# Convolution taps of a gated MLP: from an SBUF copy of the up-projection to the PSUM accumulator itself

## The chip, the cores and the metric

The kernel runs on one core of a Trainium2 chip. The core has five engines that run side by side and wait for each other on semaphores: TensorE (matrix products, into PSUM), VectorE, ScalarE and GpSimd (elementwise work) and SyncE (here: the queue that issues the DMA transfers). The profile calls them PE, DVE, ACT, POOL and SP; PEld is the loading of TensorE's weights. PSUM is TensorE's output memory; it has eight banks, and one bank holds a 128 x 512 float32 tile. GpSimd has no path to PSUM in this kernel: all that it reads lies in SBUF.

The metric is the device time of one execution in microseconds. Three runs of the kernel before gave 3285.91, 3288.57 and 3295.32 us; the median is 3288.57 us.

## The reference, cut to what matters

One layer: a mixer sub-layer (Fourier transform and gated linear recurrence, not touched here) and a gated MLP with a depthwise 3 x 3 convolution. The change lies in the MLP, which in the reference is

```python
def conv_ffn(h, w_up, conv_w, conv_b, w_down, rows, cols):
    b, l, _ = h.shape                                        # 2048 tokens = 32 rows x 64 columns
    z = (h @ w_up).reshape(b, rows, cols, 2 * D_FF)          # 1024 -> 5632 channels
    z = lax.conv_general_dilated(z, conv_w[:, :, None, :], window_strides=(1, 1), padding='SAME',
                                 dimension_numbers=('NHWC', 'HWIO', 'NHWC'),
                                 feature_group_count=2 * D_FF)   # each channel by itself
    z = z.reshape(b, l, 2 * D_FF) + conv_b
    return (jax.nn.silu(z[..., :D_FF]) * z[..., D_FF:]) @ w_down   # 2816 -> 1024
```

Its output is scaled, added to the stream and normed. All is float32.

## The kernel before

Every large product is taken in three matmuls: both operands are split into a rounded high part (a ScalarE cast, L102) and a remainder (a subtraction, L103, on GpSimd or VectorE), and hi*hi, hi*lo and lo*hi are summed in PSUM (`mm3`, L140 to L147). `load_w` (L130) brings a 1024 x 128 column tile of a weight matrix in two halves: for each half a DMA into a staging tile `rw` (two buffers), a cast and a GpSimd subtraction. The split weights have two buffers (`w`), so a weight tile can be prepared while TensorE uses the one before.

Phase 3 (`phase3`, L933) is the up-projection with the convolution. Its input, `h2`, lies in SBUF, channels on the partitions, in four blocks of 512 tokens. The 5632 channels are worked off in 44 tiles of 128: for each j from 0 to 21 first channel tile j (half 0, the part that goes through Silu) and then channel tile j + 22 (half 1, the factor). One channel tile is

- 96 matmuls (4 token blocks x 8 slices of the 1024 inputs x 3) into `z`, 128 channels x 2048 tokens, four banks of PSUM. Half 0 uses the pool `za`, half 1 `zb`, one tile each, so that TensorE can write one while the other is read.
- on ScalarE the copy `zs` of all four banks to SBUF (L952, two buffers) and from `zs` the centre tap with the bias, into `ac` (L953, three buffers).
- on VectorE the other eight taps (`conv`, L967): eight multiply-add instructions (L979), each reading a shifted view of `zs` and adding to `ac` in place.

After both halves `gate` (L961) applies Silu to `ac` of half 0 on ScalarE (L963), multiplies both halves on GpSimd (L964) and stores the product to DRAM (`dZ[j]`). For the last j, Silu, product and store are written later, in the loop of `down`, and the product is on VectorE.

`down` (L982) is the down-projection: two halves of 512 output channels times four blocks of 512 tokens, eight groups of 22 x 12 matmuls. A group sums into four tiles `dn` of one bank each, from a pool of its own that is opened when the two pools of `z` have closed. In the first group, each of its 22 steps loads and splits both a weight tile (`wd`, into the SBUF slots H0 to H5 that held `h2`) and a tile of `dZ` (`gh`, `gl`, three buffers); the weights stay for the next three groups.

Each engine works off its own queue strictly in order. That order isn't the order of the program text: a planner walks through the traced instructions with estimated durations, and puts onto each engine the earliest-traced instruction that is ready in its estimate. An instruction whose input comes later than estimated holds up all that stands behind it on its engine. `tc.issue_after(x)` adds a fixed order behind the instruction x.

Of the kernel before, what the change touches and what calls it, by code (L numbers as in the profile page):

```python
"""FNet / HGRN2 / ConvFFN hybrid layer on one Trainium2 core.

The large matrix products run in float32r: every float32 operand is split exactly into a high
part (12 significant bits) and the remainder, and hi*hi + hi*lo + lo*hi is accumulated in PSUM.
The HGRN2 recurrence runs over windows of 128 tokens; inside a window the decays between two
tokens are products of per-block prefix and suffix products at dyadic block sizes (all factors
are at most one), one product per level, merged by level masks. The FNet position transform is
a 16 x 128 factorization: 16-point transforms on VectorE, twiddled 128-point ones on TensorE.
"""
# [8 lines left out]
F32 = mybir.dt.float32  # L18
# [12 lines left out]
NB = 4            # 512-token blocks  # L31
TB = 512
KD = D // P       # 8
DFF = 2816
NF = DFF // P     # 22
# [10 lines left out]
def constants():  # L46
    """Arrays that depend on the shapes alone."""
    n2 = np.arange(128)
    # level masks: entry (s, t) belongs to the level whose block size first separates s and t
# [5 lines left out]
    cmask = np.stack(lev, 1)                       # [s, 8, t]  # L55
    # twiddled 128-point transforms, one table for each residue k1
# [13 lines left out]
    ch = np.stack([np.cos(ang), np.sin(ang)], 1) / 512.0             # [c, 2, c']  # L70
    eye = np.eye(128)
    rst = np.zeros((128, 640))
    rst[:, 127::128] = 1.0                                           # where the scans restart
# [5 lines left out]
def fap(t, off, dims):  # L79
    """Access pattern over the free elements of a whole tile."""  # L80
    a = t[:]
    return bass.AP(a.tensor, a.offset + off, [list(a.ap[0])] + [list(q) for q in dims])


class Banks:
    """PSUM tiles from the pool that holds their tag."""
# [8 lines left out]
class Layer:  # L95
# [3 lines left out]
    # ------------------------------------------------------------------ helpers  # L99
    def split(self, hi, lo, raw, eng=None):  # L100
        """hi = raw rounded to 12 bits, lo = raw - hi."""
        self.nc.scalar.copy(hi, raw)  # L102
        (eng or self.nc.gpsimd).tensor_tensor(lo, raw, hi, op=SUB)  # L103

    def load_split(self, hi, lo, src, eng=None, pool=None, bufs=2):
        """Load [128, n] or [128, k, c] float32 data of at most 512 columns and split it."""
# [10 lines left out]
    def rsqrt(self, pool, v, n):  # L117
        """v ** -0.5 for positive v of shape [128, n]: bit-level guess and three Newton steps."""
# [11 lines left out]
    def load_w(self, ap, name):  # L130
        """A [1024, 128] column tile of a weight matrix -> hi, lo tiles [128, 8, 128]."""
# [8 lines left out]
    def mm3(self, ps, pairs, start=True, stop=True):  # L140
        """Accumulate the products of the (lhs_hi, lhs_lo, rhs_hi, rhs_lo) in pairs."""
# [7 lines left out]
    # ------------------------------------------------------------------ the layer  # L149
# [44 lines left out]
    # ------------------------------------------------------------------ phase 1  # L194
    def phase1(self):
# [6 lines left out]
        self.mod_A = pc.tile([P, KD], F32, name="mod_A")       # norm1_g * (1 + scale)  # L202
# [17 lines left out]
        # the projections fill TensorE between the small products of the two branches  # L220
# [21 lines left out]
    def drain(self):  # L242
        """Trace the rest of the filler's first part and go on to the next."""
        for _ in self.filler.pop(0):
            pass

    def project_all(self, h):
        """The projections of head h for the state passes; from the second head on, with parts of the
        later modulations."""
# [8 lines left out]
    def vec_rows(self, p0):  # L258
        """Small vectors, loaded as rows of 128 and turned into columns."""
# [17 lines left out]
    def startup(self, p0):  # L277
        nc, a = self.nc, self.a
        ps = self.ps
        # silu(c), silu(c_ctx) as columns  # L280
# [7 lines left out]
        # weights of the FNet channels; one half sits where the context goes later  # L288
# [9 lines left out]

        # shift and scale of the first sub-layer, for latents and context: silu(c)^T @ ada_w; the last
        # 512 columns by VectorE, the others by TensorE  # L300
# [45 lines left out]
        # token tiles -> modulated, transposed, split; the products of a block follow the transposes of  # L346
        # the next one
# [24 lines left out]
        # softmax over the two rows of hg_lb, first row  # L372
# [14 lines left out]
        # conv taps as columns  # L387
# [10 lines left out]
    def load_x(self, p0, blk):  # L398
        """The token tiles of a block, each token scaled to unit mean square."""
# [19 lines left out]
    def modulate_steps(self, pool, xs, A, B, hi, lo, tags, every):  # L419
        """[tok, d] tiles -> transposed h = x * A[d] + B[d], split into hi and lo [d, 8, tok]."""  # L420
# [23 lines left out]
    def fill(self, n):  # L444
        """Trace up to n steps of the projections that wait in self.filler; a context in which
        TensorE's instructions are queued behind them."""
        mm = None
        for _ in range(n):
            mm = next(self.filler[0], None) or mm
        return self.tc.issue_after(mm.ins) if mm else nullcontext()  # L450

    def project_steps(self, kind, h):
        """One 128-channel tile of x @ w_in (channel-major), with its activation, to DRAM, in steps
        of three products."""
# [29 lines left out]
    # ------------------------------------------------------------------ FNet branch  # L484
# [9 lines left out]
    def fnet(self, p1, g):  # L494
        nc, a, ps = self.nc, self.a, self.ps
        X = p1.tile([P, 2, TB], F32, name="fX", tag="fX")           # blocks 0, 1 (later G0, G2)
        EF = p1.tile([P, 4, TB], F32, name="fE", tag="fE")          # e, f, g, h
        H = p1.tile([P, 16, P], F32, name="fH", tag="fH")

        U = p1.tile([P, 2, TB], F32, name="fU", tag="fU")           # blocks 2, 3  # L500
# [5 lines left out]
        # 4-point transforms over a (n1 = 4a + b); index b inside the 512 columns  # L506
        v.tensor_tensor(X[:, 0, :], EF[:, 0, :], EF[:, 1, :], op=ADD)      # G_b[0]
        v.tensor_tensor(X[:, 1, :], EF[:, 0, :], EF[:, 1, :], op=SUB)      # G_b[2]
        G0 = X[:, 0, :].rearrange("p (b c) -> p b c", b=4)
        G2 = X[:, 1, :].rearrange("p (b c) -> p b c", b=4)  # L510
        gg = EF[:, 2, :].rearrange("p (b c) -> p b c", b=4)                # Re G_b[1]
        hh = EF[:, 3, :].rearrange("p (b c) -> p b c", b=4)                # -Im G_b[1]
        S = EF[:, 0:2, :].rearrange("p x (b c) -> p (x b) c", b=4)         # scratch, 8 slots
        # H slots: 0,1: k=0,8;  2,3: k=4 (re, -im); 4,5: k=2; 6,7: k=6; 8,9: 1; 10,11: 5; 12,13: 9; 14,15: 13
        # residue 0
# [4 lines left out]
        # residue 2: X2 = G0 + r(G1-G3) - i(G2 + r(G1+G3)), X6 = G0 - r(G1-G3) - i(r(G1+G3) - G2)  # L520
# [7 lines left out]
        # residue 1: W_b = (g - i h)(cos - i sin), b = 0..3, planes re, im in W  # L528
        W = H[:, 8:16, :].rearrange("p (x b) c -> p x b c", x=2)           # [re|im][b]
# [8 lines left out]
        Sv = S.rearrange("p (q x) c -> p q x c", q=4)                      # q: A, D, C, E ; x: re, im  # L538
# [4 lines left out]
        Hk = H[:, 8:16, :].rearrange("p (k x) c -> p k x c", x=2)          # k: 1, 5, 9, 13  # L543
# [7 lines left out]
        Y = EF                                                             # e .. h are no longer needed  # L551
# [526 lines left out]
```

## Time and profile before

| what | value |
|---|---|
| median of three runs | 3288.57 us (3285.91 to 3295.32) |
| the profiled execution: span from its first to its last instruction | 3293.7 us (its own device time isn't listed beside it; the span stands within the three runs' times) |
| busy TensorE / VectorE / ScalarE / GpSimd | 3128.3 / 2007.5 / 933.0 / 957.0 us |
| mean granted TensorE clock | 0.979 of full speed |
| phase 3: first matmul of `z` to start of its last | 1699.6 to 2760.2 us |
| down-projection: start of its first and of its last L1020 matmul | 2781.5 to 3280.4 us |

How to read the lines shown below: a group row gives line, engine, operation, output <- inputs, shapes and count, then busy time and the mean duration in ns, then the idle time just before these instructions and who ended it. A row of one source line gives count, least/median/largest duration in ns, and the first and last start. A timeline row gives start and duration in us, engine, line, operation, count, and in brackets the idle time before it and who ended it. A row of stretches gives from:to, the length, then busy us and instruction counts (x) of PE, PEld, DVE, ACT and POOL, the granted clock, the DMA share and GB/s; an instruction that crosses an edge is counted in both stretches. A matmul row of 0.39 us overlaps its neighbours: the distance of two starts is what one costs.

### The profile page before, as it was taken

To read this page: it belongs to the slowest core of one execution; us is meant where nothing else is said; L and a number is where in the kernel's file an instruction comes from. 1 tells how busy PE (TensorE), PEld (TensorE's weight loads), DVE (VectorE), ACT (ScalarE), POOL (GpSimd) and SP (SyncE) were. 2 spreads that over 40 slices of the span, in tenths; PEclk is the share of its full clock that TensorE was granted. 3 is DMA by queue.
4 is the path that set the end of the run, shared out by engine and by line. 5 is a ranking of instruction groups with operands and counts; after the bars stand their busy time and mean duration, and the time that the engine had idled before them with its cause. 6 is when DMAs were issued, how large, how long until landed. Compare 5 with 4: busy or idle time off the path is not lost.

```text
span 3293.7 us, 38879 instructions
## 1 busy us (share of the span) xinstructions
PE 3128.3 (95%) x14955; PEld 2576.7 (78%) x14955; DVE 2007.5 (61%) x2538; ACT 933.0 (28%) x1498; POOL 957.0 (29%) x514
## 2 busy tenths in 40 slices
PE   7999999999999999999999999999999997999998
PEld 4977788888888888777778777777777776788886
DVE  5355543576666611566458988988988999302324
ACT  3322112233333321333232222222122122323322
POOL 2200110000000011345333434334343343544443
PEclk8999999999999999999999999999999998999999
DMA  6255654423323234555531111101111112534643
GB/s 223 85 166 182 196 166 138 134 95 102 106 90 105 86 111 145 187 165 183 178 110 36 58 36 52 48 32 51 45 36 48 45 46 72 192 121 155 220 147 131
DMA packets 278506, 372.59 MB, mean 113 GB/s; under 512 B 20253, under 2 KB 154289, under 8 KB 274993
## 3 DMA queue, kind: packets, MB, share of 16 engines
q1 hardware_dynamic: 278321, 370.11, 34.3%
q8 instruction: 118, 1.93, 0.2%
q14 instruction: 67, 0.55, 0.1%
HBM read 268.58 MB, written 101.45 MB: 112 GB/s over the span
## 4 chain that ended last, share of the span: by engine, by line
PE 49%; DVE 31%; DMA 8%; issue 5%; ACT 3%; POOL 3%; SPq 0%; ACTq 0%; DVEq 0%; POOLq 0%
DVE ac L979 27%; PE pj L145 8%; PE pj L144 8%; PE pj L146 8%; PE dn L1022 4%; PE dn L1020 4%; PE dn L1021 4%; PE pa L773 3%; ACT ac L953 1%; DMA rw<-in_w_out_dram 1%; DMA rw<-in_w_b_dram 1%; POOL wab L103 1%; PE wo L906 1%; PE wo L908 1%; PE wo L907 1%
## 5 line engine op out<-in xcount | busy, mean ns | idle before, releaser
L979 DVE SCALAR_TENSOR_TENSOR ac<-zs,cw,ac 128x1953 f32<-128x1953 f32 (+2 forms) x352 | 970.2, 2761 | 105.9 <-ACT ac L953 95.3
L146 PE MATMUL z<-h,w_up 128*128 128x512 f32 x1408 | 565.3, 402 | 58.4 <-POOL w_up L103 58.4
L144 PE MATMUL z<-h,w_up 128*128 128x512 f32 x1408 | 560.9, 398 | 1.9 <-DVE mt L912 1.9
L145 PE MATMUL z<-h,w_up 128*128 128x512 f32 x1408 | 560.2, 398 | 0.0
L146 PEld LDWEIGHTS z<-h,w_up 128*128 128x128 f32 x1408 | 272.1, 193 | 126.1 <-POOL w_up L103 69.3
L103 POOL TENSOR_TENSOR w_up<-rw,w_up 128x512 fp32r<-128x512 f32 x88 | 267.5, 3058 | 348.6 <-ACT w_up L102 348.5
L103 POOL TENSOR_TENSOR gl<-rw,gh 128x512 fp32r<-128x512 f32 x176 | 244.4, 1391 | 272.3 <-ACT gh L102 266.0
L144 PEld LDWEIGHTS z<-h,w_up 128*128 128x128 f32 x1408 | 272.6, 194 | 59.2 <-issue 2.3
L145 PEld LDWEIGHTS z<-h,w_up 128*128 128x128 f32 x1408 | 272.0, 193 | 58.4
L1020 PE MATMUL dn<-wd,gh 128*128 128x512 f32 x704 | 278.7, 396 | 22.0 <-ACT zs L952 20.9
L1022 PE MATMUL dn<-wd,gl 128*128 128x512 f32 x704 | 278.9, 396 | 4.0 <-POOL gl L103 4.0
L1021 PE MATMUL dn<-wd,gh 128*128 128x512 f32 x704 | 278.1, 395 | 0.0
L964 POOL TENSOR_TENSOR ac<-ac 128x2048 f32<-128x2048 f32 x21 | 138.8, 6609 | 274.8 <-DVE ac L979 274.8
L102 ACT CAST gh<-rw 128x512 fp32r<-128x512 f32 x176 | 109.1, 621 | 350.9 <-PE dn L1021 219.4
L952 ACT COPY zs<-z 128x2048 f32<-128x2048 f32 x44 | 82.3, 1872 | 392.2 <-PE z L146 392.2
L479 ACT ACTIVATE ev<-pj 128x512 f32<-128x512 f32 (+1 forms) x136 | 79.8, 587 | 354.0 <-PE pj L146 326.3
L1020 PEld LDWEIGHTS dn<-wd,gh 128*128 128x128 f32 x704 | 133.1, 189 | 54.0 <-ACT zs L952 21.3
L1038 DVE TENSOR_TENSOR dtmp<-dn,m 128x512 f32<-128x512 f32 x32 | 21.6, 685 | 247.2 <-PE dn L1022 247.1
L1022 PEld LDWEIGHTS dn<-wd,gl 128*128 128x128 f32 x704 | 133.0, 189 | 38.2 <-POOL gl L103 7.7
L1021 PEld LDWEIGHTS dn<-wd,gh 128*128 128x128 f32 x704 | 133.0, 189 | 30.5
L773 PEld LDWEIGHTS pa<-bQ,bkc 128*128 128x128 f32 x896 | 120.7, 191 | 16.8 <-issue 10.4
L773 PE MATMUL pa<-bQ,bkc 128*128 128x128 f32 x896 | 127.5, 286 | 1.2
(303 smaller groups left out, 6105.8 us busy)
## 6 DMA issues: line engine op xcount, KB each, us to landing
rw<-dZ SPq DMA_DIRECT2D x176, 256.0 KB, 3.1
rw<-in_ffn_up_dram SPq DMA_DIRECT2D x88, 256.0 KB, 3.0
dZ<-ac SPq DMA_DIRECT2D x22, 1024.0 KB, 3.9
rw<-in_w_in_dram SPq DMA_DIRECT2D x80, 256.0 KB, 3.2
maw<-in_ada_w_dram SPq DMA_DIRECT2D x64, 256.0 KB, 3.2
rw<-in_w_out_dram SPq DMA_DIRECT2D x64, 256.0 KB, 2.7
x<-dX SPq DMA_DIRECT2D x48, 256.0 KB, 5.3
rw<-in_ffn_down_dram SPq DMA_DIRECT2D x44, 256.0 KB, 3.1
```

Of the source, the lines that this page charges most:

```text
L102: self.nc.scalar.copy(hi, raw)
L103: (eng or self.nc.gpsimd).tensor_tensor(lo, raw, hi, op=SUB)
L144: self.nc.tensor.matmul(ps, lh, rh, start=start and i == 0, stop=False)
L145: self.nc.tensor.matmul(ps, lh, rl, start=False, stop=False)
L146: mm = self.nc.tensor.matmul(ps, ll, rh, start=False, stop=stop and i == last)
L773: mm = nc.tensor.matmul(pa[:, c], kc[:, c], fap(Q, w * P, [(2 * m, nw), (W + m, 2), (1, m)]), start=True, stop=True)
L952: nc.scalar.copy(zs, z)
L964: (nc.gpsimd if j < NF - 1 else nc.vector).tensor_tensor(acc[0], acc[0], acc[1], op=MUL)
L979: nc.vector.scalar_tensor_tensor(o, z3[:, r0 + dy:r1 + dy, c0 + dx:c1 + dx], self.cw[:, k, jj:jj + 1], o, op0=MUL, op1=ADD)
L1020: nc.tensor.matmul(accs[i], gh[:, t], wh, start=(kk == 0), stop=False)
L1021: nc.tensor.matmul(accs[i], gh[:, t], wl, start=False, stop=False)
L1022: nc.tensor.matmul(accs[i], gl[:, t], wh, start=False, stop=(kk == NF - 1))
```

## The change

- Phase 3 has no `zs` any more. The centre tap (`activation` with Identity) is done once for each of the four banks, straight from `z` in PSUM, right behind the matmuls of that bank in the program; the eight other taps read shifted views of `z` in PSUM. `ac` has four buffers in place of three.
- Silu of half 0 moves from `gate` to right behind the taps of half 0, ahead of the weight load of half 1 in the program.
- `za` and `zb` stay open through `down`, which takes its accumulators from them: a group's four banks are now one tile `dn` of 2048 columns, even groups in `za`, odd ones in `zb`.
- In the first down group the remainders of the first eight weight tiles (k < 8) are taken on GpSimd; before it was those of k = 0, 2 and 4.

The file's comments and docstrings are also gone, with blank lines in their place, so that line numbers up to phase 3 are the same. The core of the diff:

```diff
-                    ac = p5.tile([P, SEQ], F32, name="ac", tag="ac", bufs=3)
+                ac = p5.tile([P, SEQ], F32, name="ac", tag="ac", bufs=4)
...
-                        self.mm3(z[:, n * TB:(n + 1) * TB],
-                                 [(wh[:, k, :], wl[:, k, :], hh[:, k, :], hl[:, k, :]) for k in range(KD)])
-                    zs = p5.tile([P, SEQ], F32, name="zs", tag="zs", bufs=2)
-                    nc.scalar.copy(zs, z)
-                    nc.scalar.activation(ac, zs, AF.Identity, scale=self.cw[:, 4, jj:jj + 1], bias=self.v("cb", jj))
-                    self.conv(ac, zs, jj)
+                    b = slice(n * TB, (n + 1) * TB)
+                    self.mm3(z[:, b], [(wh[:, k, :], wl[:, k, :], hh[:, k, :], hl[:, k, :]) for k in range(KD)])
+                    nc.scalar.activation(ac[:, b], z[:, b], AF.Identity, scale=self.cw[:, 4, jj:jj + 1], bias=self.v("cb", jj))
+                self.conv(ac, z, jj)
+                if not half:
+                    nc.scalar.activation(ac, ac, AF.Silu)
...
     def gate(self, j, acc):
         nc = self.nc
-        nc.scalar.activation(acc[0], acc[0], AF.Silu)
...
-        with tc.tile_pool(name="ps3", bufs=1, reuse_waits="tile", space=PSUM) as ps:
+        with ExitStack() as es:
+            es.push(self.psB.__exit__)
+            es.push(self.psA.__exit__)
...
-                accs = [ps.tile([P, TB], F32, name=f"dn{i}", tag=f"dn{i}_{gi % 2}") for i in range(4)]
+                dn = (self.zb if gi % 2 else self.za).tile([P, SEQ], F32, name="dn", tag="z")
+                accs = [dn[:, i * TB:(i + 1) * TB] for i in range(4)]
...
-                                        None if gi == 0 and k in (0, 2, 4) else nc.vector, *((self.pw, 2) if gi == 0 else (p6, 4)))
+                                        None if gi == 0 and k < 8 else nc.vector, *((self.pw, 2) if gi == 0 else (p6, 4)))
```

More of the change, by code (lines that the diff above doesn't have):

```diff
@@ L934, in phase3 @@
         tc, nc, a = self.tc, self.nc, self.a
-        with ExitStack() as es:
-            es.push(self.psA.__exit__)
-            for j in range(NF):
-                acc = []
-                for half in range(2):
-                    jj = j + half * NF
-                    wh, wl = self.load_w(a["ffn_up"][0, :, jj * P:(jj + 1) * P], f"up{jj}")
-                    if jj == NF:
-                        self.psB.__exit__(None, None, None)
-                        zb = es.enter_context(tc.tile_pool(name="ps2b", bufs=1, reuse_waits="tile", space=PSUM))
-                    z = (zb if half else self.za).tile([P, SEQ], F32, name="z", tag="z")
-                    ac = p5.tile([P, SEQ], F32, name="ac", tag="ac", bufs=3)
-                    for n in range(NB):
-                        hh, hl = self.h2[n]
-                        self.mm3(z[:, n * TB:(n + 1) * TB],
-                                 [(wh[:, k, :], wl[:, k, :], hh[:, k, :], hl[:, k, :]) for k in range(KD)])
-                    zs = p5.tile([P, SEQ], F32, name="zs", tag="zs", bufs=2)
-                    nc.scalar.copy(zs, z)
-                    nc.scalar.activation(ac, zs, AF.Identity, scale=self.cw[:, 4, jj:jj + 1], bias=self.v("cb", jj))
-                    self.conv(ac, zs, jj)
-                    acc.append(ac)
-                last = lambda: self.gate(j, acc)
-                if j < NF - 1:
-                    last()
@@ new lines, in phase3 @@
+        for j in range(NF):
+            acc = []
+            for half in range(2):
+                jj = j + half * NF
+                wh, wl = self.load_w(a["ffn_up"][0, :, jj * P:(jj + 1) * P], f"up{jj}")
+                if jj == NF:
+                    self.psB.__exit__(None, None, None)
+                    self.psB = tc.tile_pool(name="ps2b", bufs=1, reuse_waits="tile", space=PSUM)
+                    self.zb = self.psB.__enter__()
+                z = (self.zb if half else self.za).tile([P, SEQ], F32, name="z", tag="z")
+                ac = p5.tile([P, SEQ], F32, name="ac", tag="ac", bufs=4)
+                for n in range(NB):
+                    hh, hl = self.h2[n]
+                    b = slice(n * TB, (n + 1) * TB)
[4 more added lines that the diff above has]
+                    nc.scalar.activation(ac, ac, AF.Silu)
+                acc.append(ac)
+            last = lambda: self.gate(j, acc)
+            if j < NF - 1:
+                last()
```

## The prediction

> **What bounds the kernel now.** I first looked for the stretches in which TensorE, 95% busy over the whole span, is not kept busy: 100 us each of phase 3, of the passage to the down-projection and of the down-projection.
>
> ```profile
> core 0: us, PE busy (x) PEld busy (x) DVE busy (x) ACT busy (x) POOL busy (x), PEclk, DMA share, GB/s
> ...
> 1900.00:2000.00 100.00, 93.67 (x393) 76.31 (x392) 90.38 (x33) 24.09 (x19) 38.38 (x10) 0.95 0.14 48
> ...
> 2700.00:2800.00 100.00, 76.92 (x324) 62.67 (x323) 94.00 (x41) 26.70 (x28) 41.20 (x14) 0.88 0.21 71
> ...
> 2900.00:3000.00 100.00, 100.00 (x432) 81.07 (x431) 10.09 (x16) 27.18 (x52) 46.47 (x36) 1.00 0.43 139
> ```
>
> In phase 3 VectorE works 90% of the time and TensorE gets 393 matmuls into 100 us; in the down-projection it gets 432. Then the timeline of one pair of channel tiles in the middle of phase 3, engine by engine (ACT, DVE, POOL, PE):
>
> ```profile
> 2127.29 1.87 ACT L952 COPY zs<-z 128x2048 f32<-128x2048 f32 x1 [16.16 <-PE z L146]
> 2145.65 1.92 ACT L963 ACTIVATE ac<-ac 128x2048 f32<-128x2048 f32 x1 [16.50 <-DVE ac L979]
> 2147.47 2.08 ACT L953 ACTIVATE ac<-zs,vt,cw 128x2048 f32<-128x2048 f32 x1
> 2149.46 1.12 ACT L102 CAST w_up<-rw 128x512 fp32r<-128x512 f32 x2
> ...
> 2100.89 44.67 DVE L979 SCALAR_TENSOR_TENSOR ac<-zs,cw,ac 128x2016 f32<-128x2016 f32 x16 [4.03 <-ACT ac L953]
> 2149.59 44.67 DVE L979 SCALAR_TENSOR_TENSOR ac<-zs,cw,ac 128x2016 f32<-128x2016 f32 x16 [4.03 <-ACT ac L953]
> ...
> 2121.26 6.60 POOL L964 TENSOR_TENSOR ac<-ac 128x2048 f32<-128x2048 f32 x1 [13.63 <-DVE ac L979]
> 2127.82 6.50 POOL L103 TENSOR_TENSOR w_up<-rw,w_up 128x512 fp32r<-128x512 f32 x2
> ...
> 2127.09 0.39 PE L144 MATMUL z<-h,w_up 128*128 128x512 f32 x1
> 2127.32 0.39 PE L145 MATMUL z<-h,w_up 128*128 128x512 f32 x1
> 2131.16 0.79 PE L146 MATMUL z<-h,w_up 128*128 128x512 f32 x1 [3.45 <-POOL w_up L103]
> 2131.75 0.63 PE L144 MATMUL z<-h,w_up 128*128 128x512 f32 x1
> 2132.18 0.63 PE L145 MATMUL z<-h,w_up 128*128 128x512 f32 x1
> ```
>
> The rhythm is VectorE's: sixteen taps take 44.67 us, then it idles 4.03 us because ScalarE does Silu (L963), which waits for those taps, ahead of the next centre tap; 2149.59 - 2100.89 = 48.70 us a pair. TensorE is held by the tail of that chain: GpSimd's product (L964) waits for taps, the weights' remainders (L103) stand behind it, and TensorE waits 3.45 us for them. After the pause it is slow: 2131.75 to 2132.18 is 0.43 us a matmul, against 0.23 before. Undisturbed, ScalarE's copies show how long TensorE needs for a tile, since they start when one ends:
>
> ```profile
> 1727.91 1.87 ACT L952 COPY zs<-z 128x2048 f32<-128x2048 f32 x1 [4.88 <-PE z L146]
> ...
> 1749.67 1.88 ACT L952 COPY zs<-z 128x2048 f32<-128x2048 f32 x1 [16.87 <-PE z L146]
> ...
> 1814.95 1.88 ACT L952 COPY zs<-z 128x2048 f32<-128x2048 f32 x1 [7.28 <-PE z L146]
> ```
>
> That is 21.76 us a tile (four tiles in 87.04 us), 43.52 a pair: 5.2 us less than the rhythm. Last, TensorE's waits after 1699 us, and the first and last starts of two lines:
>
> ```profile
> PE z L146 <- POOL w_up L103: 58.4, 23, 4.1
> PE dn L1020 <- ACT zs L952: 20.9, 1, 20.9
> PE dn L1022 <- POOL gl L103: 4.0, 7, 0.9
> ...
> L146 PE MATMUL z<-h,w_up x1408: 387/389/796, 1699.6 to 2760.2; 128*128 128x512 f32 x176
> ...
> L1020 PE MATMUL dn<-wd,gh x704: 389/393/796, 2781.5 to 3280.4; 128*128 128x512 f32 x176
> ```
>
> The 20.9 us are the passage: `down` may open its PSUM only when the last `z` has been copied, and that copy waits for a `zs` buffer, which VectorE, a tile behind, still reads.
>
> **Step 1: what the taps cost from PSUM.** What makes VectorE slow is visible in the spread of its instructions while GpSimd works beside it. L879, L912, L1038 and L824 read one operand from PSUM and one from SBUF; L881 and L979 read two from SBUF; the last row is GpSimd's.
>
> ```profile
> L879 DVE TENSOR_TENSOR gt<-pj,gt x64: 675/682/694, 1301.2 to 1599.0; 128x512 f32<-128x512 f32 x64
> L912 DVE TENSOR_TENSOR mt<-wo,m x32: 675/683/692, 1366.8 to 1698.2; 128x512 f32<-128x512 f32 x32
> L1038 DVE TENSOR_TENSOR dtmp<-dn,m x32: 673/684/693, 2849.8 to 3281.4; 128x512 f32<-128x512 f32 x32
> L824 DVE SCALAR_TENSOR_TENSOR bg<-pt,vt,bg x16: 729/730/752, 655.1 to 1169.5; 128x512 f32<-128x512 f32 x16
> ...
> L881 DVE TENSOR_TENSOR gt<-gt x32: 674/692/1651, 1302.6 to 1599.7; 128x512 f32<-128x512 f32 x32
> L979 DVE SCALAR_TENSOR_TENSOR ac<-zs,cw,ac x352: 2240/2285/6549, 1732.3 to 2812.1; 128x1953 f32<-128x1953 f32 x88, 128x2016 f32<-128x2016 f32 x44, 128x1984 f32<-128x1984 f32 x44
> ...
> L103 POOL TENSOR_TENSOR w_up<-rw,w_up x88: 1268/3259/3313, 1692.8 to 2737.4; 128x512 fp32r<-128x512 f32 x88
> ```
>
> 128 instructions with a PSUM operand (L879, L912, L1038) never exceed 694 ns, though GpSimd was at work 46% of the down-projection's stretch above; the same operation from SBUF alone reaches 1651 ns, and a tap 6549 ns. The least and median are equal from both memories. So a tap should cost its undisturbed time:
>
> ```profile
> 2783.97 2.32 DVE L979 SCALAR_TENSOR_TENSOR ac<-zs,cw,ac 128x2016 f32<-128x2016 f32 x1 [0.82 <-ACT ac L953]
> 2791.79 2.27 DVE L979 SCALAR_TENSOR_TENSOR ac<-zs,cw,ac 128x1984 f32<-128x1984 f32 x1
> 2799.50 2.24 DVE L979 SCALAR_TENSOR_TENSOR ac<-zs,cw,ac 128x1953 f32<-128x1953 f32 x1
> ```
>
> A tile has two taps of each of the first two shapes and four of the third: 2 x 2.32 + 2 x 2.27 + 4 x 2.24 = 18.1 us in place of 44.67 / 2 = 22.3. No row shows VectorE reading shifted rows across four banks. Bounds: 18.1 us, and 22.3 if the collisions stay; I take 18.1, as the three PSUM rows lie at the undisturbed value. GpSimd gains too (1268 ns a remainder in place of 3259), off the path.
>
> [...]
>
> **Step 2: the new wait.** `z` is now held until its eighth tap, not until a 1.87 us copy; behind TensorE's first matmul into those banks stands the whole rest of phase 3. The centre tap of the fourth bank ends about 0.9 us after the tile's last matmul, by the same form on the same shape:
>
> ```profile
> L429 ACT ACTIVATE h<-pt,mod_B,mod_A x32: 773/779/782, 1407.0 to 1722.2; 128x512 fp32r<-128x512 f32 x32
> ```
>
> (0.78 us and some 0.1 for the signals.) Three of the four lie beside matmuls; ScalarE does 4 x 0.78 = 3.1 us a tile in place of 1.87 + 2.08. The banks are free 0.9 + 18.1 = 19.0 us after the tile's end, and wanted after 21.76, the length of the tile in the other pool: 2.7 us to spare. VectorE, 18.1 of 21.76 us, no longer sets the rhythm. Silu becomes ready at 19.0 us, 1.92 us long, before the next fourth centre tap at 21.76. GpSimd has 4 x 1.3 + 6.6 = 11.8 us in a pair of 43.5, and the remainders have a full tile of time, as weights have two buffers. So TensorE runs through: from 1727.9, 43 tiles x 21.76 = 935.7, end at 2663.6 in place of 2760.6 (the last start 2760.2 and 0.39). That is 97.0 us: 58.4 of waits and 38.6 of slow matmuls behind them. The fourth `ac` buffer costs nothing, `zs` leaves its room. All this needs the four banks of `z` to be followed separately, as the two halves of a weight tile are: TensorE began at 2131.16 with the first remainder of two (2127.82, 6.50 us for both).
>
> **Step 3: the passage.** The first group takes `za`, whose taps ended during the last tile: the 20.9 us go. The second wants `zb` a group later. One tile in place of four costs nothing: its readers (L1038, 4 x 0.68 us) are hidden by the 61 us of the group in the other pool; uncovered they would cost 2.7 us in each of six groups. The first group is limited by its loads:
>
> ```profile
> 2804.00:2865.00 61.00, 55.82 (x233) 42.52 (x232) 27.36 (x21) 20.37 (x37) 34.39 (x22) 1.00 0.65 211
> 2865.00:2926.00 61.00, 61.00 (x264) 49.48 (x263) 5.05 (x8) 16.13 (x30) 28.32 (x22) 1.00 0.45 146
> ...
> 2744.32 1.14 ACT L102 CAST wd<-rw 128x512 fp32r<-128x512 f32 x2 [1.43 <-PE z L146]
> ```
>
> 31 matmuls fewer than a group's 264, at 61.0 / 264 = 0.23 us: 7.2 us lost, and some 2.6 us of slow start before (13 matmuls x 0.2). The slow start goes; but the weights can't be cast before the first block of the last tile is done (the third row: 2760.6 - 2744.3 = 16.3 us ahead), and now no 20.9 us of standstill follow in which eight were readied, only 16.3 us. Eight remainders on GpSimd, 2 x 1.3 us a step with `gl`, fit under 12 x 0.23 = 2.8 us, and VectorE is free of taps after 19 us, before k = 8 is wanted at 22. Bounds: the group ends 10 us earlier or 21 us later by itself; I take the two as equal, 0.
>
> **The sum.** -97.0 - 20.9 = -117.9 us. On the profiled span, 3293.7 - 117.9 = 3175.8; on the median of the runs, 5.1 us below that span, 3288.6 - 117.9 = **3170 us**. The other seven groups and the end are the same.
>
> **The rivals.**
> (B) The taps still collide, or reading shifted rows in PSUM is slower: a tile then takes (21.76 + 0.9 + 22.3) / 2 = 22.5 us, as TensorE and VectorE take turns on two sets of banks; 43 x 0.7 = +31: 3201 us. It begins to count at 20.9 us for eight taps. For it: the untested pattern; against it: the three rows.
> (C) The standstill moves: TensorE arrives 97 us earlier, but finds no weights and waits as long as before: 3170 + 21 = 3191. For it: DMA at 211 GB/s in that stretch; against it: 16.3 us of lead.
> (D) It doesn't do what it says: remainders still stand behind GpSimd's product, which the planner orders, and TensorE keeps the 48.7 us rhythm: 3288.6 - 20.9 - 2.6 = 3265.
> (E) Slower: Silu, now traced ahead of half 1's weights, stands ahead of their casts on ScalarE. TensorE would idle after each half 0 for 0.9 + 18.1 + 1.92 + 0.62 (cast) + 1.27 (remainder) = 22.8 us and start slowly (2.6): 43.5 + 25.4 = 68.9 a pair, 22 x 20.2 = +444, less 20.9: 3712 us. It turns the sign from 118 / 22 = 5.4 us of idle a pair. For it: ScalarE stood 16.50 us before Silu, with casts behind it (2149.46). Against it: two weight buffers let the casts be planned a tile ahead, and Silu's input should come about when planned once taps don't collide.
>
> (F) `z` is followed as one tile: TensorE waits for the centre tap after each of three banks, 3 x 0.9 x 44 = +119 us: 3289. For it: no row has a PSUM tile written and read by banks; against it: the half weight tile.
>
> **Chances.** Forecast 0.64, B 0.09, C 0.10, D 0.10, E 0.05, F 0.02. The forecast's own spread is about 3155 to 3185 (step 3's gain, a few us of small waits); with B and C the range 3152 to 3215 holds eight in ten, D, E and F stay out. About 0.3% (10 us, the spread of the three runs) can be told from no change. Faster: 0.64 + 0.09 + 0.10 + 0.09 of D = 0.92; same: F and the rest of D, 0.03; slower: E, 0.05.
>
> **What would show it.** Step 1: L979 with a largest value near 2.4 us, none at 3 or 6.5, and GpSimd's remainders near 1.27. Step 2: ends of tiles 21.8 us apart to the last, no wait of `z` matmuls for L979 or L103, 1.00 clock, and DVE busy some 83%. Step 3: the first L1020 right behind the last L146 near 2664. A wait of TensorE for L979 speaks for B, for the casts L102 for E, for remainders L103 in phase 3 for D, at the passage for C.

## The result: slower, and the profile after

| | before | after |
|---|---|---|
| median of the runs (four each) | 3287.99 us (3285.91 to 3295.32) | 3346.65 us (3342.86 to 3347.19) |
| the profiled execution's span | 3293.7 us | 3345.2 us |
| mean granted TensorE clock | 0.979 | 0.989 |

The ratio is 1.0171 (95% interval 1.0151 to 1.0191): the change makes the kernel 1.7% slower, where 3170 us was forecast. Line numbers of the changed kernel: centre tap L952, Silu L955, product L964, taps L979, `dn` matmuls L1023 to L1025, first reader of `dn` L1041.

A stretch of the changed kernel in the middle of phase 3 (columns as in the rows of stretches of before):

```profile
core 0: us, PE busy (x) PEld busy (x) DVE busy (x) ACT busy (x) POOL busy (x), PEclk, DMA share, GB/s
2192.00:2292.00 100.00, 89.45 (x381) 70.09 (x379) 71.60 (x33) 19.52 (x25) 18.58 (x10) 1.00 0.12 39
```

VectorE fell from 90% to 72%, the clock is at 1.00 in this stretch, and still TensorE does fewer matmuls than before: 381 in place of 393 per 100 us. So VectorE no longer sets the rhythm, and something else does. TensorE's waits in phase 3 and after it (total us, times, longest) name it:

```profile
engine line waited for: us in total, times, longest us
PE z L144 <- ACT ac L952: 116.8, 129, 3.6
PE z L144 <- ACT h L429: 5.2, 1, 5.2
```

The 58.4 us of waits for the remainders L103 and the 20.9 us at the passage are gone. In their place stand 129 waits for the centre tap: three for each of 43 tiles, all but the first. The timeline (ACT, DVE, PE) shows one of them:

```profile
2189.81 0.78 ACT L952 ACTIVATE ac<-z,vt,cw 128x512 f32<-128x512 f32 x1 [5.84 <-PE z L146]
...
2195.25 0.78 ACT L952 ACTIVATE ac<-z,vt,cw 128x512 f32<-128x512 f32 x1 [3.63 <-PE z L146]
2201.86 0.78 ACT L952 ACTIVATE ac<-z,vt,cw 128x512 f32<-128x512 f32 x1 [5.83 <-PE z L146]
...
2215.09 0.78 ACT L952 ACTIVATE ac<-z,vt,cw 128x512 f32<-128x512 f32 x1 [3.92 <-PE z L146]
...
2190.70 18.46 DVE L979 SCALAR_TENSOR_TENSOR ac<-z,cw,ac 128x2016 f32<-128x2016 f32 x8 [6.97 <-ACT ac L952]
...
2194.82 0.39 PE L146 MATMUL z<-h,w_up 128*128 128x512 f32 x1
2196.08 0.50 PE L144 MATMUL z<-h,w_up 128*128 128x512 f32 x1 [0.87 <-ACT ac L952]
2196.42 0.39 PE L145 MATMUL z<-h,w_up 128*128 128x512 f32 x1
```

The centre tap at 2189.81 is a tile's last. The next comes 5.44 us later, which is the time of 24 undisturbed matmuls; the one after that 6.61 us later, and 2215.09, again a tile's last, is two steps of 6.62 us further on. So within a tile TensorE stands still until the centre tap of the bank it has just finished has ended, and only then begins the next bank; between two tiles, which lie in different pools, it does not. A pause costs 1.18 us: the idle 0.87 us, 0.16 us in which matmuls would have overlapped (2196.08 - 2194.82 = 1.26, less 0.23 for a matmul and 0.87), and some 0.15 us of slower restart (0.34 us to the next start in place of 0.23, and a little behind it). The taps themselves are as fast as hoped, and the product on GpSimd too (rows of source lines of the changed kernel: count, least/median/largest ns, first and last start):

```profile
L979 DVE SCALAR_TENSOR_TENSOR ac<-z,cw,ac x352: 2243/2264/2321, 1737.6 to 2851.4; 128x1953 f32<-128x1953 f32 x88, 128x2016 f32<-128x2016 f32 x44, 128x1984 f32<-128x1984 f32 x44
...
L964 POOL TENSOR_TENSOR ac<-ac x21: 4591/4602/4615, 1778.9 to 2790.9; 128x2048 f32<-128x2048 f32 x21
...
L146 PE MATMUL z<-h,w_up x1408: 387/389/632, 1692.5 to 2827.6; 128*128 128x512 f32 x176
...
L1023 PE MATMUL dn<-wd,gh x704: 387/392/628, 2827.9 to 3326.3; 128*128 128x512 f32 x176
```

With the rows of L146 and L1023 the two spans can be set against each other, part by part:

| part | before | after | difference |
|---|---|---|---|
| ahead of phase 3 (not changed; between 1692.5 and 1701.1 us in the runs here) | 1699.6 | 1692.5 | -7.1 |
| phase 3, first to last start of L146 | 1060.6 | 1135.1 | +74.5 |
| passage to the first `dn` matmul | 21.3 | 0.3 | -21.0 |
| down-projection, first to last start of its first line | 498.9 | 498.4 | -0.5 |
| from there to the end | 13.3 | 18.9 | +5.6 |
| span | 3293.7 | 3345.2 | +51.5 |

### The profile page after: what moved, and what is told of

Same layout as the page of the kernel before. It is cut to its first block, busy times and chain, and to the rows that moved or that the text cites. A ratio compares the mean times of both kernels' runs of the same rounds, so it can differ in the third digit from the quotient of the medians.

```text
span 3345.2 us, 38901 instructions
## 1 busy us (share of the span) xinstructions
PE 3137.2 (94%) x14955; PEld 2550.1 (76%) x14955; DVE 1829.6 (55%) x2533; ACT 896.2 (27%) x1586; POOL 754.1 (23%) x519
## 4 chain that ended last, share of the span: by engine, by line
PE 75%; DMA 7%; ACT 5%; DVE 4%; issue 2%; POOL 2%; SPq 0%; ACTq 0%; DVEq 0%; POOLq 0%
PE z L144 10%; PE z L146 9%; PE z L145 9%; PE pj L144 8%; PE pj L146 8%; PE pj L145 8%; PE dn L1025 4%; PE dn L1023 4%; PE dn L1024 4%; PE pa L773 3%; ACT ac L952 3%; DMA rw<-in_w_b_dram 1%; DMA rw<-in_ffn_down_dram 1%; DMA rw<-in_w_out_dram 1%; PE wo L906 1%
## 5 line engine op out<-in xcount | busy, mean ns | idle before, releaser
L979 DVE SCALAR_TENSOR_TENSOR ac<-z,cw,ac 128x1953 f32<-128x1953 f32 (+2 forms) x352 | 801.2, 2276 | 321.8 <-ACT ac L952 311.1
L144 PE MATMUL z<-h,w_up 128*128 128x512 f32 x1408 | 565.5, 402 | 123.9 <-ACT ac L952 116.8
L146 PE MATMUL z<-h,w_up 128*128 128x512 f32 x1408 | 551.4, 392 | 0.0
L145 PE MATMUL z<-h,w_up 128*128 128x512 f32 x1408 | 551.2, 391 | 0.0
L144 PEld LDWEIGHTS z<-h,w_up 128*128 128x128 f32 x1408 | 265.7, 189 | 231.1 <-ACT ac L952 171.9
L952 ACT ACTIVATE ac<-z,vt,cw 128x512 f32<-128x512 f32 x176 | 137.0, 778 | 863.6 <-PE z L146 863.6
L146 PEld LDWEIGHTS z<-h,w_up 128*128 128x128 f32 x1408 | 265.7, 189 | 57.0
L145 PEld LDWEIGHTS z<-h,w_up 128*128 128x128 f32 x1408 | 265.8, 189 | 52.1
L103 POOL TENSOR_TENSOR gl<-rw,gh 128x512 fp32r<-128x512 f32 x176 | 236.6, 1346 | 278.8 <-ACT gh L102 277.0
L1025 PE MATMUL dn<-wd,gl 128*128 128x512 f32 x704 | 279.2, 397 | 3.2 <-POOL gl L103 3.1
L1023 PE MATMUL dn<-wd,gh 128*128 128x512 f32 x704 | 278.5, 396 | 0.8 <-ACT gh L102 0.8
L103 POOL TENSOR_TENSOR w_up<-rw,w_up 128x512 fp32r<-128x512 f32 x88 | 112.5, 1301 | 541.1 <-ACT w_up L102 541.1
L102 ACT CAST gh<-rw 128x512 fp32r<-128x512 f32 x176 | 108.6, 619 | 265.0 <-PE dn L1024 201.1
L964 POOL TENSOR_TENSOR ac<-ac 128x2048 f32<-128x2048 f32 x21 | 96.7, 4604 | 324.2 <-DVE ac L979 324.2
L1041 DVE TENSOR_TENSOR dtmp<-dn,m 128x512 f32<-128x512 f32 x32 | 20.8, 681 | 263.6 <-PE dn L1025 263.6
L1025 PEld LDWEIGHTS dn<-wd,gl 128*128 128x128 f32 x704 | 132.7, 188 | 38.3 <-POOL gl L103 7.1
L1023 PEld LDWEIGHTS dn<-wd,gh 128*128 128x128 f32 x704 | 132.8, 189 | 32.3 <-ACT gh L102 1.7
```

The source lines that it names most:

```text
L144: self.nc.tensor.matmul(ps, lh, rh, start=start and i == 0, stop=False)
L145: self.nc.tensor.matmul(ps, lh, rl, start=False, stop=False)
L146: mm = self.nc.tensor.matmul(ps, ll, rh, start=False, stop=stop and i == last)
L952: nc.scalar.activation(ac[:, b], z[:, b], AF.Identity, scale=self.cw[:, 4, jj:jj + 1], bias=self.v("cb", jj))
L964: (nc.gpsimd if j < NF - 1 else nc.vector).tensor_tensor(acc[0], acc[0], acc[1], op=MUL)
L979: nc.vector.scalar_tensor_tensor(o, z3[:, r0 + dy:r1 + dy, c0 + dx:c1 + dx], self.cw[:, k, jj:jj + 1], o, op0=MUL, op1=ADD)
```

## The experiments

The theory, T: whoever sets the waits of the program follows `z` as one tile. A matmul that writes bank n + 1 waits for an earlier instruction that reads bank n, since both touch `z`. The rival, R: the waits are the chip's: while ScalarE reads one bank of PSUM, TensorE is held from the other banks of that pool, however the banks are followed. Beside these the runs ask what step 2 and step 3 of the prediction are worth by themselves. All ratios are to the kernel before, run on the same chip (medians 3289.70 us for the first four, 3290.99 us for the others).

| run | median (range), us | ratio (95% interval) | span |
|---|---|---|---|
| four centre taps behind all banks | 3197.54 (3192.01 to 3200.44) | 0.9712 (0.9696 to 0.9728) | 3198.6 |
| one centre tap | 3179.39 (3177.24 to 3182.38) | 0.9663 (0.9649 to 0.9677) | 3180.6 |
| two centre taps of two banks | 3257.48 (3255.87 to 3258.87) | 0.9899 (0.9885 to 0.9914) | 3254.6 |
| phase 3 of before, `down` of after | 3302.46 (3300.07 to 3308.70) | 1.0039 (1.0024 to 1.0054) | 3299.7 |
| `z` as four one-bank tiles, copied | 3282.49 (3275.68 to 3294.40) | 0.9974 (0.9960 to 0.9987) | 3292.6 |
| one centre tap, last down group in four tiles | 3174.40 (3171.42 to 3181.14) | 0.9641 (0.9620 to 0.9663) | 3172.4 |
| one centre tap, `down` of before | 3196.51 (3194.74 to 3197.52) | 0.9706 (0.9683 to 0.9728) | 3193.9 |

### Four centre taps, traced behind the matmuls of all four banks

```diff
                     self.mm3(z[:, b], ...)
-                    nc.scalar.activation(ac[:, b], z[:, b], AF.Identity, ...)
+                for n in range(NB):
+                    b = slice(n * TB, (n + 1) * TB)
+                    nc.scalar.activation(ac[:, b], z[:, b], AF.Identity, ...)
                 self.conv(ac, z, jj)
```

> The four centre taps stay one per bank, but stand in the program behind the matmuls of all four banks. Theory T (the tracing layer follows z as one: the first matmul of a bank waits for the centre tap that was traced before it, whatever bank that tap reads; 3 waits a tile, 21.76 + 3 x 1.18 = 25.3 us a tile in the changed kernel): no wait of TensorE inside a tile, so the centre taps of the first three banks run beside matmuls if a read is followed bank by bank (tile 21.8 us, 3160 to 3180 us), or all four stand behind the last matmul if a read too is followed as one (4 x 0.78 + 18.5 = 21.6 us against 21.76 in the other pool, with Silu in between: tile 21.8 to 23 us, 3170 to 3230 us). Rival R (ScalarE's read of PSUM beside matmuls itself holds TensorE up): TensorE still pauses near each centre tap, tile 25 us, 3330 to 3350 us.

Measured: 3197.54 us, 149 us less than the changed kernel. The same instructions do the same work; only the place of the four in the program text differs. The trace shows both why the gain is large and why it stops short of the next run. Its timeline (ACT) and its waits of TensorE (here the centre tap is L954, the taps are L981):

```profile
2126.35 2.79 ACT L954 ACTIVATE ac<-z,vt,cw 128x512 f32<-128x512 f32 x4 [16.66 <-PE z L146]
```

```profile
PE z L144 <- DVE ac L981: 13.0, 11, 2.4
```

No wait for a centre tap is left. The four now run in one go, after ScalarE has idled 16.66 us until the tile's last matmul, though three of the four banks were finished long before: a read of one bank waits for the writes of all. That is T in the other direction. The pauses are gone, but the four instructions take 2.79 us where one takes 2.06 (next run), and that is too much for VectorE: for a pair of tiles it needs two times 18.46 us of taps, and stands for one Silu (1.92 us) and for two centre taps in between, 18.46 x 2 + 1.92 + 2 x 2.79 = 44.4 us against TensorE's 43.52. Hence the waits for the taps, and 18 us above the next run.

### One centre tap of 2048 columns

```diff
-                    nc.scalar.activation(ac[:, b], z[:, b], AF.Identity, ...)
+                nc.scalar.activation(ac, z, AF.Identity, ...)
                 self.conv(ac, z, jj)
```

> One centre tap of 2048 columns from PSUM behind all four banks, all else as in the changed kernel. Theory T: no wait inside a tile; the taps end 2.2 + 18.5 = 20.7 us after the tile, TensorE wants the banks after 21.76: tile 21.8 us, phase 3 about 100 us shorter than before, 3160 to 3185 us. Rival R as above: at most one pause a tile, 3220 to 3260 us. Rival S (Silu ahead of the next centre tap on ScalarE makes VectorE late): TensorE waits for L979, tile 22 to 23 us, 3180 to 3230 us.

Measured: 3179.39 us, 0.9663 of the time before, 167 us less than the changed kernel. Its stretch in the middle of phase 3, then its timeline (ACT, DVE, PE), then the row of its third matmul line:

```profile
2200.00:2300.00 100.00, 100.00 (x443) 82.67 (x442) 82.99 (x38) 19.05 (x17) 26.50 (x13) 1.00 0.16 53
```

```profile
2118.02 2.06 ACT L952 ACTIVATE ac<-z,vt,cw 128x2048 f32<-128x2048 f32 x1 [18.01 <-PE z L146]
...
2138.67 1.92 ACT L955 ACTIVATE ac<-ac 128x2048 f32<-128x2048 f32 x1 [17.57 <-DVE ac L979]
2140.49 2.05 ACT L952 ACTIVATE ac<-z,vt,cw 128x2048 f32<-128x2048 f32 x1
...
2161.57 2.07 ACT L952 ACTIVATE ac<-z,vt,cw 128x2048 f32<-128x2048 f32 x1 [18.00 <-PE z L146]
...
2142.57 18.46 DVE L979 SCALAR_TENSOR_TENSOR ac<-z,cw,ac 128x2016 f32<-128x2016 f32 x8 [3.99 <-ACT ac L952]
...
2161.31 0.39 PE L144 MATMUL z<-h,w_up 128*128 128x512 f32 x1
```

```profile
L146 PE MATMUL z<-h,w_up x1408: 387/389/478, 1697.0 to 2661.8; 128*128 128x512 f32 x176
```

This is the forecast's phase 3: TensorE runs through, 443 matmuls per 100 us at the full clock, 2661.8 - 1697.0 = 964.8 us, 95.8 less than before. The margin is thin. VectorE ends a pair's second taps at 2142.57 + 18.46 = 2161.03, and TensorE's next tile into the banks that they read begins at 2161.31: 0.3 us. The run before shows what happens when 0.7 us more is asked for each tile.

### Two centre taps of two banks each

```diff
-                    nc.scalar.activation(ac[:, b], z[:, b], AF.Identity, ...)
+                    if n % 2:
+                        b = slice((n - 1) * TB, (n + 1) * TB)
+                        nc.scalar.activation(ac[:, b], z[:, b], AF.Identity, ...)
```

> Two centre taps of 1024 columns, after the second and the fourth bank. Theory T: one wait a tile instead of three, for a tap of about 1.2 us and the restart: tile 21.76 + 1.6 = 23.4 us, 44 x 1.9 = 85 us less than the changed kernel: 3255 to 3270 us. Rival R: pauses follow the read columns, which are the same: 3330 to 3350 us.

Measured: 3257.48 us, 78 us above the run with one centre tap. The waits and the timeline of this kernel (ACT, PE; the centre tap is L954):

```profile
PE z L144 <- ACT ac L954: 58.2, 43, 2.6
```

```profile
2207.58 1.21 ACT L954 ACTIVATE ac<-z,vt,cw 128x1024 f32<-128x1024 f32 x1 [8.64 <-PE z L146]
...
2208.84 0.50 PE L144 MATMUL z<-h,w_up 128*128 128x512 f32 x1 [1.30 <-ACT ac L954]
```

One pause a tile in place of three: one behind each centre tap that has matmuls of its own tile after it. Each is as long as its centre tap and 0.1 us: 1.30 for 1.21 here, 0.87 for 0.78 in the changed kernel. ScalarE reads as many columns of PSUM in each tile as in the changed kernel, so the pauses don't go by the columns read in all. This run doesn't yet tell T from R: R too would hold TensorE only while a read lies between matmuls of the same pool, and that is one read of 1.21 us a tile here, three of 0.78 us in the changed kernel.

### `z` as four tiles of one bank, copy and centre tap for each bank

```diff
-                z = (self.zb if half else self.za).tile([P, SEQ], F32, name="z", tag="z")
+                zt = [(self.zb if half else self.za).tile([P, TB], F32, name=f"z{n}", tag=f"z{n}") for n in range(NB)]
+                zs = p5.tile([P, SEQ], F32, name="zs", tag="zs", bufs=2)
...
-                    self.mm3(z[:, b], ...)
-                    nc.scalar.activation(ac[:, b], z[:, b], AF.Identity, ...)
-                self.conv(ac, z, jj)
+                    self.mm3(zt[n], ...)
+                    nc.scalar.copy(zs[:, b], zt[n])
+                    nc.scalar.activation(ac[:, b], zt[n], AF.Identity, ...)
+                self.conv(ac, zs, jj)
```

(and `dn` as four one-bank tiles in the same pools; `ac` with three buffers). Taps reach over the banks' edges, so with four tiles they need the copy.

> z as four separate tiles of one bank; for each bank, right behind its matmuls, ScalarE copies it to zs and takes the centre tap from PSUM; the eight taps read zs in SBUF as in the kernel before (three ac buffers). The down-projection uses the same one-bank tiles, the first eight weight remainders stay on GpSimd. Theory T (z is followed tile by tile): though ScalarE reads each bank twice while TensorE writes the next, TensorE has no pause between banks; the taps collide with GpSimd again (L979 up to 6.5 us, 44.7 us of taps a pair), VectorE sets a rhythm of 45 to 48.7 us a pair: 3190 to 3280 us. Rival R (a ScalarE read beside matmuls holds TensorE): pauses after each of the first three banks, 25 us a tile, 3330 us or more.

Measured: 3282.49 us, 0.9974 of before. This run decides between T and R: it reads each bank right behind its matmuls, as the changed kernel does, twice even, from the same PSUM banks. Its timeline near the start of phase 3 (ACT: copy L953, centre tap L954), where nothing else holds TensorE yet, its waits of TensorE, and the row of its taps:

```profile
1738.59 0.59 ACT L953 COPY zs<-z 128x512 f32<-128x512 f32 x1 [3.14 <-PE z L146]
1739.07 0.79 ACT L954 ACTIVATE ac<-z,vt,cw 128x512 f32<-128x512 f32 x1
...
1744.03 0.59 ACT L953 COPY zs<-z 128x512 f32<-128x512 f32 x1 [4.17 <-PE z L146]
```

```profile
PE z L146 <- POOL w_up L103: 47.7, 23, 4.1
```

```profile
L981 DVE SCALAR_TENSOR_TENSOR ac<-zs,cw,ac x352: 2239/2285/6551, 1734.5 to 2801.9; 128x1953 f32<-128x1953 f32 x88, 128x2016 f32<-128x2016 f32 x44, 128x1984 f32<-128x1984 f32 x44
```

Banks end 5.44 us apart, the undisturbed time, with ScalarE reading the bank before for 1.3 us of each; no wait of TensorE for the centre tap or the copy is in the list. R falls: the read beside the matmuls costs nothing. Two things separate this kernel from the changed one here: each bank is a tile of its own, and the taps read the copy. Taps that read PSUM don't hold TensorE by themselves, as the run with one centre tap shows (443 matmuls per 100 us), so the tiles are what is left, and T stands. The kernel isn't fast for two reasons. Its taps read two operands from SBUF and reach 6.55 us (in the kernel before, the tap of 6.54 us at 2123.45 lies beside GpSimd's product, 6.60 us from 2121.26, and the remainder behind it), and TensorE waits for the remainders L103 as before: phase 3 is 13.7 us shorter than before (1701.1 to 2748.0 us). And the down-projection is 31 us longer (529.8 us between the starts of its first line, 498.9 before), with 17.3 us of waits for casts of `gh`, as in the next run. The median lies 2.5 us above the range that was given for T.

### Phase 3 of before, with the `down` of after

```diff
-                ac = p5.tile([P, SEQ], F32, name="ac", tag="ac", bufs=4)
+                ac = p5.tile([P, SEQ], F32, name="ac", tag="ac", bufs=3)
...
-                    nc.scalar.activation(ac[:, b], z[:, b], AF.Identity, ...)
-                self.conv(ac, z, jj)
-                if not half:
-                    nc.scalar.activation(ac, ac, AF.Silu)
+                zs = p5.tile([P, SEQ], F32, name="zs", tag="zs", bufs=2)
+                nc.scalar.copy(zs, z)
+                nc.scalar.activation(ac, zs, AF.Identity, ...)
+                self.conv(ac, zs, jj)
```

(and Silu in `gate` again).

> Phase 3 as before (copy zs, one centre tap from it, three ac buffers, Silu behind both halves), the down-projection as changed (accumulators in the two pools of z, first eight weight remainders on GpSimd). Step 3 of the prediction: the 20.9 us standstill and its slow restart go, 3262 to 3272 us. Rival C (the standstill only moves to the loads of the first group): 3280 to 3292 us.

Measured: 3302.46 us, ratio 1.0039, so a little slower, above both expectations. Its timeline (ACT, PE; the copy is L951, Silu L962):

```profile
2781.28 1.86 ACT L951 COPY zs<-z 128x2048 f32<-128x2048 f32 x1
2783.04 1.91 ACT L962 ACTIVATE ac<-ac 128x2048 f32<-128x2048 f32 x1
...
2786.83 1.13 ACT L102 CAST gh<-rw 128x512 fp32r<-128x512 f32 x2
...
2753.35 0.39 PE L1022 MATMUL dn<-wd,gh 128*128 128x512 f32 x1
2757.26 0.80 PE L1023 MATMUL dn<-wd,gh 128*128 128x512 f32 x1 [3.53 <-POOL wd L103]
...
2787.49 0.79 PE L1022 MATMUL dn<-wd,gh 128*128 128x512 f32 x1 [19.21 <-ACT gh L102]
```

The standstill isn't removed but moved. The first `dn` matmuls start at once (2753.35), but the next casts of `gh` stand on ScalarE behind the late copy of the last `z`, its Silu and its centre tap, and TensorE waits 19.21 us for them, after 3.53 us for a remainder. What is late now is the input of the down-projection, not its PSUM. In the kernels that read `z` from PSUM no copy is late, so this queue doesn't form: there the passage took 0.3 us. The rest, some 6 us, is the end: the same edit makes it longer, which the next run takes up.

### One centre tap, and the last down group in four one-bank tiles

The changed kernel's last 18.9 us are 5.6 longer than before's 13.3. The timelines (DVE) of before and of the changed kernel, at the first read of the last group's sums:

```profile
3272.97 0.69 DVE L1038 TENSOR_TENSOR dtmp<-dn,m 128x512 f32<-128x512 f32 x1 [34.75 <-PE dn L1022]
```

```profile
3327.16 1.29 DVE L1041 TENSOR_TENSOR dtmp<-dn,m 128x512 f32<-128x512 f32 x2 [40.53 <-PE dn L1025]
```

Before read the first of four sums 7.4 us ahead of its last `dn` matmuls (L1020 ends its starts at 3280.4); the changed kernel reads it only after its last (3326.3). T would say why: `dn` is one tile. The kernel of this run is that with one centre tap, but for the last group, for which `zb` closes and a pool with four one-bank tiles opens (left out below: the centre tap, and a line that closes the new pool at the end):

```diff
...
-                dn = (self.zb if gi % 2 else self.za).tile([P, SEQ], F32, name="dn", tag="z")
-                accs = [dn[:, i * TB:(i + 1) * TB] for i in range(4)]
+                if gi == 2 * NB - 1:
+                    self.psB.__exit__(None, None, None)
+                    self.psB = tc.tile_pool(name="ps3b", bufs=1, reuse_waits="tile", space=PSUM)
+                    zt = self.psB.__enter__()
+                    accs = [zt.tile([P, TB], F32, name=f"dl{i}", tag=f"dl{i}") for i in range(4)]
+                else:
+                    dn = (self.zb if gi % 2 else self.za).tile([P, SEQ], F32, name="dn", tag="z")
+                    accs = [dn[:, i * TB:(i + 1) * TB] for i in range(4)]
```

> As e2_one_after, but the last group of the down-projection sums into four separate one-bank tiles. Theory T: in e2_one_after the first reader of the last group's accumulators starts after its last matmul, in the kernel before 8 us ahead of it, and the end after the last matmul takes 18.5 us instead of 12.9; here again 12.9: 5.6 us less than e2_one_after, 3171 to 3177 us. Rival (the end is limited by the loads and stores at the output): no change, 3178 to 3182 us.

Measured: 3174.40 us, 5.0 less than with one centre tap alone, as expected; the ranges of the two overlap, so the trace has to decide. Its timeline (DVE, PE):

```profile
3151.64 0.69 DVE L1047 TENSOR_TENSOR dtmp<-dl,m 128x512 f32<-128x512 f32 x1 [31.97 <-PE dl L1031]
...
3159.57 0.40 PE L1031 MATMUL dl<-wd,gl 128*128 128x512 f32 x1
```

VectorE reads the first sum 7.9 us ahead of the last matmul again, and from the start of that matmul to the end of the span it is 3172.4 - 3159.57 = 12.8 us; with one centre tap alone it is 18.5 (3180.6 - 3162.1). This is the fastest of the kernels: 0.9641 of before, 172 us less than the changed kernel.

### One centre tap, with the `down` of before

```diff
-            es.push(self.psB.__exit__)
-            es.push(self.psA.__exit__)
+            self.psA.__exit__(None, None, None)
+            self.psB.__exit__(None, None, None)
+            ps = es.enter_context(tc.tile_pool(name="ps3", bufs=1, reuse_waits="tile", space=PSUM))
...
-                dn = (self.zb if gi % 2 else self.za).tile([P, SEQ], F32, name="dn", tag="z")
-                accs = [dn[:, i * TB:(i + 1) * TB] for i in range(4)]
+                accs = [ps.tile([P, TB], F32, name=f"dn{i}", tag=f"dn{i}_{gi % 2}") for i in range(4)]
```

(and one centre tap as above, and the remainders k = 0, 2, 4 on GpSimd, not k < 8).

> Phase 3 as in e2_one_after (one centre tap, taps from PSUM), the down-projection as in the kernel before: a PSUM pool of its own with one-bank tiles, opened when both z pools have closed, remainders of k = 0, 2, 4 on GpSimd. Step 3 holds: TensorE stands still until the last tile's taps end, 2.1 + 18.5 = 20.6 us, restarts slowly (2.6), and the end is 5.6 us shorter: 3179 + 17.6 = 3190 to 3202 us. Rival C (the loads of the first group bound the passage anyway): 3172 to 3182 us.

Measured: 3196.51 us. Its timeline (PE):

```profile
2685.10 0.77 PE L1023 MATMUL dn<-wd,gh 128*128 128x512 f32 x1 [24.13 <-DVE ac L979]
2685.67 0.63 PE L1024 MATMUL dn<-wd,gh 128*128 128x512 f32 x1
```

With a pool of its own, `down` stands 24.13 us until the last taps have read `z`, and starts slowly after it. Against the run above, which differs by the `down` alone and has nearly the same end, the edit of `down` is worth 3196.51 - 3174.40 = 22.1 us. That is a net figure: the passage is 24 us longer here, and the down-projection behind it 3 us shorter (495.7 us from its first matmul to its last, 498.7 above). That weights made ready during the standstill shorten it would fit step 3 of the prediction, but no run shows it.

## Why the prediction was wrong, step by step

**Step 1 was right.** A tap from PSUM takes 2264 ns in the median, 2321 at most, where before had 2285 and 6549; eight take 18.46 us (18.1 predicted, without the gaps between them). So reading shifted rows across four banks costs nothing extra here, and rival B's collisions don't occur. GpSimd gained as said, and more: remainders take 1301 ns in the mean (the row below, from the groups of the changed kernel), the product 4.60 us in place of 6.61.

```profile
L103 POOL TENSOR_TENSOR w_up<-rw,w_up 128x512 fp32r<-128x512 f32 x88 | 112.5, 1301 | 541.1 <-ACT w_up L102 541.1
```

A copy to SBUF ahead of the eight taps gains nothing here: the copied taps of the run with one-bank tiles are no faster in the median (2285 ns against 2264), and the slowest takes 6551 ns, 4.2 us more than the slowest from PSUM (2321).

**Step 2 failed, at one sentence:** "All this needs the four banks of `z` to be followed separately, as the two halves of a weight tile are". They are not: a matmul into one bank waits for ScalarE's read of another (129 waits), and a read of one bank waits for the matmuls of all (16.66 us of idle on ScalarE in the run with four centre taps behind all banks). The half weight tile was a row about SBUF and about two separately loaded halves; no row of before had a PSUM tile written and read bank by bank, as the prediction itself said for rival F. All else in step 2 held: without the pauses phase 3 shrank by 95.8 us, 97.0 predicted, at 83% VectorE, with no wait for L979 in TensorE's list but one of 1.0 us:

```profile
PE z L144 <- DVE ac L979: 1.0, 1, 1.0
```

Only the slack was narrower: 0.3 us at the end of a pair in the run with one centre tap, where 2.7 us a tile was worked out, since the centre tap of all four banks, Silu and the next centre tap stand in VectorE's way one after the other.

**Rival F happened, and its size was off.** Three pauses a tile, but mostly at 1.18 us each, not 0.9: the overlap of matmuls that is lost and the restart weren't counted. From a tile's last centre tap to the next tile's it is 2215.09 - 2189.81 = 25.28 us, 3.52 more than the undisturbed 21.76. The waits lie in 43 of the 44 tiles. In 42 of them that makes 148 us; the last tile takes 2828.07 - 2796.89 = 31.18 us, 9.4 more than undisturbed, because two of its centre taps stand on ScalarE behind casts of the down-projection's weights (ACT; the second of the two):

```profile
2796.89 0.78 ACT L952 ACTIVATE ac<-z,vt,cw 128x512 f32<-128x512 f32 x1 [5.83 <-PE z L146]
...
2818.49 0.62 ACT L102 CAST wd<-rw 128x512 fp32r<-128x512 f32 x1 [1.41 <-DMA rw<-in_ffn_down_dram]
2819.01 0.77 ACT L952 ACTIVATE ac<-z,vt,cw 128x512 f32<-128x512 f32 x1
...
2828.07 0.78 ACT L952 ACTIVATE ac<-z,vt,cw 128x512 f32<-128x512 f32 x1 [4.44 <-PE z L146]
```

Together that is 157 us, against the 119 of F. The difference decides the sign: 119 gives back the gain of 118, 157 gives back more. Phase 3 is 1135.1 - 964.8 = 170.3 us longer than with one centre tap, so 13 us are left beside these pauses. They lie in the first tile, which has no such wait (the changed kernel, PE and ACT):

```profile
1698.59 0.39 PE L146 MATMUL z<-h,w_up 128*128 128x512 f32 x1
...
1715.24 0.80 PE L144 MATMUL z<-h,w_up 128*128 128x512 f32 x1 [5.18 <-ACT h L429]
...
1715.09 0.77 ACT L952 ACTIVATE ac<-z,vt,cw 128x512 f32<-128x512 f32 x1
```

The tile's first bank ends after 1698.59, and then for 16.65 us TensorE starts no matmul of `z`, only the transposes (L426) that prepare the rest of `h2`. With one centre tap it runs matmuls of `z` between these transposes. The first bank's centre tap comes only at 1715.09, behind that preparation on ScalarE (L429). That the matmuls of the second bank had to be ordered behind this late centre tap would be T once more, but it isn't shown: the trace names L429 for the last 5.18 us. No term of the prediction covers this start. On the forecast's span of 3175.8 us the account is +157 for the pauses, +13 at the start of phase 3, +1 for a gain of 95.8 and not 97.0, +5.6 at the end, -7.1 for phase 3 beginning earlier and -0.6 in the passage and the down-projection: 3345 us, as measured (3345.2).

**Step 3** was right on the passage, but only together with step 2. The 20.9 us go, and the first group loses nothing against before (498.4 us of down-projection against 498.9); in the last run, where the standstill stays, it is worth 22.1 us net. By itself the same edit only moves the wait to the casts of `gh`, which step 3 didn't foresee. That standstill resembles rival C's, but it came from the late copy, not from missing weights. "One tile in place of four costs nothing" was wrong for the last of eight groups: there no other group hides the readers, and the four sums that end one after the other are read only when the last has ended, 5.6 us. The same mistake as in step 2, at another place; the prediction priced readers that come late, but not readers that are kept from coming early.

**The other rivals:** D (48.7 us rhythm through the remainders) and E (casts behind Silu) left no trace: TensorE's list has no wait for weights, L103 or L102, in phase 3. The chance of 0.02 for F was too small. Its "against" rested on one SBUF row, and all of step 2 hung on it.

## What to carry to other kernels

Before work is cut into finer pieces on one tile, find out by what unit the program's waits follow that tile: here a reader of one bank held the writer of the next, and every additional piece was a pause of mostly 1.18 us on the engine that sets the end. If the unit is the tile, read it once, behind the last write, or give each piece a tile of its own where no reader needs them joined. Reading straight from PSUM was the right idea for VectorE's taps; a single instruction on another engine, put where the program text seemed to ask for it, turned -3.4% into +1.7%.

## What the runs showed of the hardware that was not expected

The short pauses of these runs didn't bring the slow matmuls that followed longer ones. After 0.87 us (changed kernel) and 1.30 us (two centre taps) of idle time the first matmul was followed in 0.34 us and the granted clock stayed at 1.00 in the middle of phase 3; after 2.70 us (the run with one-bank tiles, PE) matmuls came 0.43 us apart for some 3 us:

```profile
2127.86 0.79 PE L146 MATMUL z<-h,w_up 128*128 128x512 f32 x1 [2.70 <-POOL w_up L103]
2128.45 0.63 PE L144 MATMUL z<-h,w_up 128*128 128x512 f32 x1
2128.88 0.63 PE L145 MATMUL z<-h,w_up 128*128 128x512 f32 x1
...
2130.90 0.39 PE L144 MATMUL z<-h,w_up 128*128 128x512 f32 x1
```

The length alone doesn't decide how many come slowly: in the kernel before, after 4.11 us of idle time (1886.74) eight steps from one matmul to the next were of 0.41 to 0.43 us, after 3.45 us (2131.16) eleven of 0.42 or 0.43. With its short pauses the changed kernel has the better mean clock (0.989 against 0.979) and still the longer time. And one ScalarE instruction over four banks of PSUM takes 2.06 us, where four over one bank each take 2.79 us back to back. These 0.73 us mattered here, because VectorE had 0.3 us to spare.
